# Memory loads in two rooms, their squares issued later, and the first side weights in the weights' own buffers

## The chip, the cores and the metric

The kernel runs on one core of one Trainium2 chip. The time is device microseconds of one execution. Three runs of the kernel before took 1450.09 to 1451.76 us, with a median of 1451.42 us. Engines are named as the profile names them: PE is TensorE (PEld its weight loads), DVE is VectorE, ACT is ScalarE, POOL is GpSimd, and SP is SyncE, whose queue (SPq) issues nearly all DMAs.

## What is computed

One layer of a hybrid encoder on 1024 tokens of width 1024, in float32, in three residual steps. The change lies in the first two.

```
h = x + W_out [ FoX(xn) ++ GLA(xn) ]        xn = RMSNorm(x); one projection W_in feeds both groups
h = h + CrossAttn(RMSNorm(h), RMSNorm(mem)) # 4 heads, QK-norm, 256 memory tokens, weights wq, wkv, wo
y = h + W2 relu(W1 RMSNorm(h))^2            # hidden 4096
```

FoX is causal attention with forget gates, 8 heads of 64, swept over blocks of 128 queries. GLA is gated linear attention, 4 heads. The keys and values of the memory tokens, `memn @ wkv`, depend on `mem` alone, so they can be computed at any time before the cross attention.

## The kernel before, in words

Every float32 product is made of three fp32r products: both operands are split into a high part (rounded, by ACT) and a low part (the rest, by DVE), and PE adds high·high, high·low and low·high (lines 110 to 112, `gemm`). A weight goes through `wsplit`: a DMA brings two blocks of 128 rows into a buffer `raw`, ACT writes `wh` (line 88 without a gain, line 99 with one), DVE writes `wl` (lines 93 and 100). All `wh` and `wl` come from one pool with nine buffers of each.

`raw` buffers come from two places. The weights' own pool (`rawp`, two buffers) exists from the start of the program. With the argument `rooms`, `wsplit` takes every other `raw` from the pool that it is given, as `raw0`. For the side work below that is the pool `side`, which takes the memory of the mixer's inputs: it exists only when PE has done its last product with them. In the trace that is at about 324 us.

The program runs in stages: the mixer's projections with GLA inside (to about 325 us, the values of FoX being the last projection, `W_FV`), the attention of FoX (to about 556 us), the output projection, the cross attention, and the MLP. During FoX a generator `side_work` is stepped between the attention blocks and gives PE further products: first `out_part(0)` (GLA's half of the output projection, left columns: weights `w_out`, split by line 838/839 of the mixer's result `mixg`, stored as `hpd`), then the memory's keys and values (four pieces of `wkv`), then `out_part(1)`.

For the memory, `side_work` loads the transposed memory `memT` in two halves and splits each half into `sh` and `sl` (line 757, done at line 120/121). It also loads the rows of `mem`, takes the mean of their squares on ACT (`mean_square`, line 136) and from it the factors `mev` and `mr` on POOL. All four loads use one buffer `memr`, so each waits for the use of the one before. The product `gx` of two gains (line 747, DVE) is needed when the first keys are scaled (line 783).

The attention itself goes: scores on PE into one of two PSUM banks `s1`, `s2` (660 to 663), row maximum `nm` on DVE (665), exponential `p` on ACT (668), reciprocal `rrec` on DVE (670), scaling on POOL (671), transposes on PE into one of three banks `tr` (696), their split into `pth` (ACT, 117) and `ptl` (DVE, 118), products with the values `va` on PE (704). The values are written to DRAM as `vd` (line 600) and read back as `va` (line 723). The buffers `pth` and `ptl` lie where the values' staging tiles `qn` were, so the first of them waits until the last `vd` store has landed.

The order of the instructions on each engine is fixed when the program is built, by a scheduler that lays the program out with its own estimate of durations. Each engine then takes its rows in that order. `issue_after(x)` tells the scheduler to place what follows behind instruction x.

Of the kernel before, what the change touches and what calls it, by code (L numbers as in the profile page):

```python
# [17 lines left out]
F32 = mybir.dt.float32  # L18
# [3 lines left out]
AF = mybir.ActivationFunctionType  # L22
ALU = mybir.AluOpType
# [5 lines left out]
D = 1024  # L29
M = 256  # L30
P = 128
# [3 lines left out]
EPS = 1e-6  # L35
# [12 lines left out]
def f(ap):  # L48
    return ap.bitcast(F32)


class Layer:
# [14 lines left out]
    def wsplit(self, src, gcols, N=512, lo_pool=0, hi_pool=False, steps=None, beside=None, rooms=None, nraw=2):  # L67


        nc = self.nc  # L70
        kt = src.shape[0] // P
        hs, ls = [], []
        for k0, n in steps or [(k, 2) for k in range(0, kt, 2)]:
            if beside is not None:
                beside(k0, n)
            self.nr += 1
            raw = (self.T(self.rawp, [P, 2, N], F32, "raw") if rooms is None or nraw == 2 and self.nr % 2
                   else self.T(rooms, [P, 2, N], F32, "raw0", bufs=nraw))
            eng = nc.scalar if beside is not None and k0 == 0 else nc.sync
            self.raw_load = eng.dma_start(raw[:, 0:n], src[k0 * P:(k0 + n) * P, :].rearrange("(k p) n -> p k n", p=P))  # L80
            for j in range(n):
                wp = self.wps[self.nw % len(self.wps)]
                self.nw += 1
                wh = self.T(wp, [P, N], F32R, "wh")
                wl = self.T(wp, [P, N], F32R, "wl")
                r = raw[:, j, :]
                if gcols is None:
                    nc.scalar.activation(wh, r, AF.Copy)
                    if lo_pool and (k0 + j) % lo_pool == 0:
                        for c in (slice(0, N // 2), slice(N // 2, N)):  # L90
                            nc.gpsimd.tensor_tensor(wl[:, c], r[:, c], f(wh[:, c]), ALU.subtract)
                    else:
                        nc.vector.tensor_tensor(wl, r, f(wh), ALU.subtract)
                else:
                    g = self.cols[:, gcols + k0 + j:gcols + k0 + j + 1]
                    if hi_pool:
                        nc.gpsimd.tensor_scalar(wh, r, g, 1.0, ALU.mult, ALU.mult)
                    else:
                        nc.scalar.activation(wh, r, AF.Identity, scale=g)  # L99
                    nc.vector.scalar_tensor_tensor(wl, r, g, f(wh), ALU.mult, ALU.subtract)  # L100
                hs.append(wh)
                ls.append(wl)
        return hs, ls
# [169 lines left out]
    def mixer_inputs(self):  # L273
        nc = self.nc
        w_in = self.w_in
        with ExitStack() as st:
# [17 lines left out]

            def token_major(t, W):
                ps = next(banks)
                self.gemm(ps, *([v[t // 4][:, k, t % 4 * P:(t % 4 + 1) * P] for k in range(KT)] for v in (xh, xl)), *W)
                return ps
# [3 lines left out]

            def normed(t, W, dst, g=None):

                ps = token_major(t, W)
                v3 = lambda ap: ap.rearrange("p (h d) -> p h d", h=8)
# [19 lines left out]
            with ExitStack() as s2:  # L326
# [14 lines left out]
                def factors(t):  # L341
# [8 lines left out]
                gbanks = self.two(mmp, 3, trp, 2)  # L350
                W = self.wsplit(w_in[:, W_GQ:W_GQ + 512], C_MIX, hi_pool=True,
                                steps=[(0, 1), (1, 1), (2, 2), (4, 2), (6, 2)], beside=columns(0), rooms=xp, nraw=5)
                ps4 = [next(gbanks) for _ in range(4)]
                for k in range(KT):
                    for i in range(4):
                        wc = slice(i * P, (i + 1) * P)
                        self.gemm(ps4[i], *([w[k][:, wc]] for w in W), *([xs(v, 0, k)] for v in (xh, xl)),
                                  start=k == 0, stop=k == KT - 1)
# [380 lines left out]
    def side_work(self, mp, mmp, trp):  # L739


        nc = self.nc
        v2 = lambda ap: ap.rearrange("p (h d) -> p h d", h=2)
        gk = self.T(mp, [P, 256], F32, "gxk")
        nc.sync.dma_start(self.gx, self.xq_g.partition_broadcast(P))
        nc.sync.dma_start(gk, self.xk_g.partition_broadcast(P))
        nc.vector.scalar_tensor_tensor(self.gx, self.gx, 0.0625, gk, ALU.mult, ALU.mult)
        yield from self.out_part(mp, mmp, 0, ())

        mh, ml = ([self.T(mp, [P, 4, P], F32R, n, bufs=6) for _ in range(4)] for n in ("sh", "sl"))  # L750
        gm = self.cols[:, C_MEM:C_MEM + 8]
        for t in range(2):
            c1 = slice(t, t + 1)
            xt = self.T(mp, [P, 4, M], F32, "memr")
            nc.sync.dma_start(xt, self.memT[:, 4 * t:4 * t + 4, :])
            for j in range(4):
                k, c = 4 * t + j, slice(2 * (j % 2), 2 * (j % 2) + 2)
                self.evac_split(mh[k // 2][:, c, :], ml[k // 2][:, c, :], xt[:, j, :].rearrange("p (t s) -> p t s", t=2), gm[:, k:k + 1])
            xt = self.T(mp, [P, D], F32, "memr")
            nc.sync.dma_start(xt, self.mem[t * P:(t + 1) * P, :])  # L760
            self.mean_square(xt, xt, self.mv[:, c1])
            nc.gpsimd.tensor_scalar(self.mev[:, c1], self.mv[:, c1], EPS, None, ALU.mult)
            nc.gpsimd.tensor_tensor(self.mr[:, c1], self.mv[:, c1], self.mhalf[:, 0:1], ALU.pow)
            yield
        for n in range(4):
            W = self.wsplit(self.wkv[:, n * 512:(n + 1) * 512], None, rooms=mp)
            for t in range(2):
                ps = self.T(mmp, [P, 512], F32, "mm")
                self.gemm(ps, *([m[k // 2][:, 2 * (k % 2) + t, :] for k in range(KT)] for m in (mh, ml)), *W)
                kv = self.T(mp, [P, 2, 512], F32R, "mkv", bufs=2)  # L770
                if n >= 2:
                    vr = self.T(mp, [P, 512], F32, "t2k", bufs=3)
                    nc.scalar.activation(vr, ps, AF.Identity, scale=self.mr[:, t:t + 1])
                    self.evac_split(kv[:, 0, :], kv[:, 1, :], vr)
                    nc.sync.dma_start(self.vmd[:, :, t, (n - 2) * 512:(n - 1) * 512], f(kv))
                    yield
                    continue
                kn = self.T(mp, [P, 512], F32, "t2k", bufs=3)
                kr = self.T(mp, [P, 512], F32, "t2k", bufs=3)
                nc.scalar.activation(kr, ps, AF.Copy)  # L780
                r = self.head_rstd(kr, kn, 2, self.mev[:, t:t + 1])
                nc.vector.tensor_tensor(v2(kn), v2(kr), self.bcast(r, 256), ALU.mult)
                nc.gpsimd.tensor_tensor(v2(kn), v2(kn), self.gx.unsqueeze(1).to_broadcast([P, 2, 256]), ALU.mult)
                yield
                tp = self.T(trp, [P, 512], F32, "tr")
                for j in range(4):
                    nc.tensor.transpose(tp[:, j * P:(j + 1) * P], kn[:, j * P:(j + 1) * P], self.ident)
                self.evac_split(kv[:, 0, :], kv[:, 1, :], tp)
                nc.sync.dma_start(self.kTd[:, :, 4 * n:4 * n + 4, t * P:(t + 1) * P],
                                  f(kv).rearrange("p s (a b) -> p s a b", a=4))  # L790

        yield from self.out_part(mp, mmp, 1, range(2))

    def out_part(self, mp, mmp, n, ks):


        nc = self.nc
        cs = slice(n * 512, (n + 1) * 512)
        W = self.wsplit(self.w_out[512:1024, cs], None, rooms=mp)
        if ks:  # L800
            W = [a + b for a, b in zip(W, self.wsplit(self.w_out[ks[0] * P:(ks[-1] + 1) * P, cs], None, rooms=mp))]
        for half in range(2):
            A = self.split_half(mp, self.mixg, half, 6, range(4))
            if ks:
                A = [a + b for a, b in zip(A, self.split_half(mp, self.mixf, half, 6, ks))]
            for i in range(4):
                ps = self.T(mmp, [P, 512], F32, "mm")
                c = slice(i * P, (i + 1) * P)
                self.gemm(ps, *([w[:, c] for w in w_] for w_ in W), *A)
                xt = self.T(mp, [P, 512], F32, "t2k", bufs=3)  # L810
                nc.sync.dma_start(xt, self.xT[:, 4 * n + i, half * 512:(half + 1) * 512])
                nc.vector.tensor_tensor(xt, ps, xt, ALU.add)
                nc.sync.dma_start(self.hpd[half, 4 * n + i], xt)
                yield
# [539 lines left out]
```

## Time and profile before

| what | value |
|---|---|
| median of three runs | 1451.42 us (1450.09 to 1451.76) |
| profiled execution | 1449.57 us, of which the span of the page is 1447.9 us |
| PE busy | 1425.1 us (98%) |
| DVE, ACT, POOL busy | 938.8 us (65%), 675.2 us (47%), 380.5 us (26%) |
| DMA | 223.93 MB, 155 GB/s mean |
| mean clock granted to PE | 0.994 of full |

The page gives busy time as a share of the span. PE is nearly always busy, so what can be won lies in the few stretches in which it waits or runs at a lower clock. These are found by the windows view (busy time and clock by stretch) and the timelines (what an engine waited for before each instruction, in square brackets).

### The profile page before, as it was taken

The numbers are of one execution on the slowest core, as the hardware profiler recorded it, in microseconds if no ns is written. First come the engines' busy times: TensorE is split into PE (matmuls) and PEld (weight loads), VectorE is DVE, ScalarE is ACT, GpSimd is POOL, SyncE is SP. The second block draws the span as 40 slices with busy tenths as digits, with TensorE's granted clock in tenths as the row PEclk, the third lists the DMA queues.
The fourth block names the chain that finished last, engine by engine and source line by source line (L and its number), as shares of the span: only waits on it lengthen the run. The fifth ranks groups of instructions, "written<-read, shape, count | busy, mean of one in ns | idle before, by whom it ended". The sixth has DMA issues, their size and how long they took to land.

```text
span 1447.9 us, 19165 instructions
## 1 busy us (share of the span) xinstructions
PE 1425.1 (98%) x7036; PEld 1188.0 (82%) x7036; DVE 938.8 (65%) x1342; ACT 675.2 (47%) x1095; POOL 380.5 (26%) x404
## 2 busy tenths in 40 slices
PE   9999999998899999999999999999999999999998
PEld 7788788887788887888888888888888888888887
DVE  5366733428687776656654886655556968778696
ACT  3443441326577755455542264445446745335230
POOL 3235423412233222512212200000000552233454
PEclk9999999999999999999999999999999999999999
DMA  8335520268567634412474114444445835436353
GB/s 312 92 71 134 134 74 0 84 166 269 173 196 210 202 124 138 139 59 88 142 263 184 44 66 175 175 174 189 175 174 207 320 127 189 132 124 225 117 201 119
DMA packets 121165, 223.93 MB, mean 155 GB/s; under 512 B 8912, under 2 KB 54512, under 8 KB 118512
## 3 DMA queue, kind: packets, MB, share of 16 engines
q1 hardware_dynamic: 119776, 218.25, 46.6%
q10 hardware_dynamic: 1296, 4.46, 1.0%
q8 instruction: 56, 0.92, 0.3%
q14 instruction: 37, 0.30, 0.1%
HBM read 150.59 MB, written 72.09 MB: 154 GB/s over the span
## 4 chain that ended last, share of the span: by engine, by line
PE 89%; DMA 5%; ACT 2%; DVE 2%; issue 1%; POOL 0%; SPq 0%; ACTq 0%; DVEq 0%
PE mm L110 15%; PE mm L111 15%; PE mm L112 15%; PE my L110 7%; PE my L112 7%; PE my L111 7%; PE tr L112 4%; PE tr L110 4%; PE tr L111 4%; PE pv L704 2%; PE tr L696 1%; PE s L660 1%; PE s L661 1%; DMA raw<-in_w_in_dram 1%; DMA raw<-in_xattn_wkv_dram 1%
## 5 line engine op out<-in xcount | busy, mean ns | idle before, releaser
L110 PE MATMUL my<-x,g 128*128 128x512 f32 x464 | 180.6, 390 | 0.2 <-ACT h L1197 0.2
L111 PE MATMUL my<-x,g 128*128 128x512 f32 x464 | 180.6, 389 | 0.0
L112 PE MATMUL my<-x,g 128*128 128x512 f32 x464 | 180.5, 389 | 0.0
L111 PE MATMUL mm<-wl,xh 128*128 128x512 f32 x320 | 126.6, 396 | 0.6 <-DVE wl L100 0.6
L110 PE MATMUL mm<-wh,xh 128*128 128x512 f32 x320 | 125.8, 396 | 0.4 <-ACT wh L99 0.3
L112 PE MATMUL mm<-wh,xl 128*128 128x512 f32 x320 | 125.7, 393 | 0.0
L1082 ACT ACTIVATE g<-s 128x1024 fp32r<-128x1024 f32 (+1 forms) x72 | 69.1, 964 | 99.9 <-PE my L112 36.5
L1083 DVE TENSOR_TENSOR g<-raw,g 128x512 fp32r<-128x512 f32 (+3 forms) x72 | 69.2, 964 | 67.9 <-ACT g L1082 67.8
L1082 ACT ACTIVATE g<-raw 128x512 fp32r<-128x512 f32 (+3 forms) x72 | 55.5, 773 | 106.1 <-DMA raw<-in_mlp_w_dram 41.9
L110 PEld LDWEIGHTS my<-x,g 128*128 128x128 f32 x464 | 87.1, 188 | 18.6 <-ACT h L1197 0.6
L111 PEld LDWEIGHTS my<-x,g 128*128 128x128 f32 x464 | 87.1, 188 | 18.3 <-DVE x L1083 0.2
L112 PEld LDWEIGHTS my<-x,g 128*128 128x128 f32 x464 | 87.1, 188 | 18.1
L1109 POOL TENSOR_TENSOR s<-raw 128x384 f32<-128x384 f32 (+1 forms) x20 | 26.4, 1318 | 280.6 <-DMA raw<-in_mlp_w_dram 253.7
L671 POOL TENSOR_SCALAR p<-p,rrec 128x128 f32<-128x128 f32 (+3 forms) x64 | 51.4, 808 | 156.5 <-DVE rrec L670 142.7
L1083 DVE TENSOR_TENSOR g<-s,g 128x1024 fp32r<-128x1024 f32 (+1 forms) x72 | 84.9, 1181 | 9.1 <-ACT g L1082 8.2
L1252 DVE TENSOR_TENSOR x<-x 128x1024 fp32r<-128x1024 f32 (+1 forms) x64 | 77.4, 1230 | 16.0 <-ACT x L1251 15.2
L111 PE MATMUL mm<-x,g 128*128 128x512 f32 x220 | 85.7, 389 | 0.0
L110 PE MATMUL mm<-x,g 128*128 128x512 f32 x220 | 85.6, 389 | 0.0
L112 PE MATMUL mm<-x,g 128*128 128x512 f32 x220 | 85.6, 389 | 0.0
L110 PE MATMUL tr<-x,g 128*128 128x512 f32 x212 | 82.5, 389 | 0.0
L111 PE MATMUL tr<-x,g 128*128 128x512 f32 x212 | 82.5, 389 | 0.0
L112 PE MATMUL tr<-x,g 128*128 128x512 f32 x212 | 82.5, 389 | 0.0
(316 smaller groups left out, 3670.6 us busy)
## 6 DMA issues: line engine op xcount, KB each, us to landing
ud<-h SPq DMA_DIRECT2D x32, 768.0 KB, 3.8
x<-ud SPq DMA_DIRECT2D x48, 512.0 KB, 5.0
raw<-in_mlp_w_dram SPq DMA_DIRECT2D x20, 1024.0 KB, 7.4
raw<-in_mlp_w_dram SPq DMA_DIRECT2D x16, 768.0 KB, 6.2
raw<-in_w_in_dram SPq DMA_DIRECT2D x23, 512.0 KB, 6.8
raw<-in_xattn_wkv_dram SPq DMA_DIRECT2D x16, 512.0 KB, 7.3
od<-o SPq DMA_DIRECT2D x32, 256.0 KB, 4.0
ud<-h SPq DMA_DIRECT2D x32, 256.0 KB, 3.3
```

Source lines behind the costliest of these rows:

```text
L110: mm(ps, lh[k], rh[k], start=start and k == 0, stop=False, **kw)
L111: mm(ps, lh[k], rl[k], start=False, stop=False, **kw)
L112: mm(ps, ll[k], rh[k], start=False, stop=stop and k == n - 1, **kw)
L660: nc.tensor.matmul(ps[:, c], qa[:, ts], ka[:, c], start=True, stop=False)
L661: nc.tensor.matmul(ps[:, c], qb[0:68, ts], kb[0:68, c], start=False, stop=not last)
L671: nc.gpsimd.tensor_scalar(p[:, 0:n], p[:, 0:n], rr, 1.0, ALU.mult, ALU.mult)
L696: t = nc.tensor.transpose(tp[:, c * P:(c + 1) * P], pp[i][:, (2 * b + j) * P:(2 * b + j + 1) * P], self.ident)
L704: nc.tensor.matmul(pv[:, 256 - (js.stop - js.start):256], va[:, 2 * b + j, :], w[:, js], start=b == j == 0 and w is th, stop=b == sb and j ...
L1082: a = self.nc.scalar.activation(hi, src, AF.Copy)
L1083: d = self.nc.vector.tensor_tensor(lo, src, f(hi), ALU.subtract)
L1109: eng.tensor_tensor(s[:, 0], raw[:, 3], raw[:, 2], ALU.add)
L1252: nc.vector.tensor_tensor(lo, f(lo), f(hi), ALU.subtract)
```

## The change

```diff
@@ wsplit @@
-                    nc.scalar.activation(wh, r, AF.Copy)
+                    self.wsplit_hi = nc.scalar.activation(wh, r, AF.Copy).ins
...
-                        nc.vector.tensor_tensor(wl, r, f(wh), ALU.subtract)
+                        self.wsplit_lo = nc.vector.tensor_tensor(wl, r, f(wh), ALU.subtract).ins
@@ side_work @@
-        nc.vector.scalar_tensor_tensor(self.gx, self.gx, 0.0625, gk, ALU.mult, ALU.mult)
         yield from self.out_part(mp, mmp, 0, ())
...
         for t in range(2):
-            c1 = slice(t, t + 1)
-            xt = self.T(mp, [P, 4, M], F32, "memr")
+            xt = self.T(mp, [P, 4, M], F32, "memr", bufs=2)
             nc.sync.dma_start(xt, self.memT[:, 4 * t:4 * t + 4, :])
...
-            xt = self.T(mp, [P, D], F32, "memr")
-            nc.sync.dma_start(xt, self.mem[t * P:(t + 1) * P, :])
-            self.mean_square(xt, xt, self.mv[:, c1])
-            nc.gpsimd.tensor_scalar(self.mev[:, c1], self.mv[:, c1], EPS, None, ALU.mult)
-            nc.gpsimd.tensor_tensor(self.mr[:, c1], self.mv[:, c1], self.mhalf[:, 0:1], ALU.pow)
             yield
+        rows = []
+        for t in range(2):
+            rows.append(self.T(mp, [P, D], F32, "memr", bufs=2))
+            nc.sync.dma_start(rows[t], self.mem[t * P:(t + 1) * P, :])
         for n in range(4):
             W = self.wsplit(self.wkv[:, n * 512:(n + 1) * 512], None, rooms=mp)
+            if n == 0:
+                with self.tc.issue_after(self.wsplit_hi), self.tc.issue_after(self.wsplit_lo):
+                    nc.vector.scalar_tensor_tensor(self.gx, self.gx, 0.0625, gk, ALU.mult, ALU.mult)
+                    for t in range(2):
+                        c1 = slice(t, t + 1)
+                        self.mean_square(rows[t], rows[t], self.mv[:, c1])
+                        nc.gpsimd.tensor_scalar(self.mev[:, c1], self.mv[:, c1], EPS, None, ALU.mult)
+                        nc.gpsimd.tensor_tensor(self.mr[:, c1], self.mv[:, c1], self.mhalf[:, 0:1], ALU.pow)
@@ out_part @@
-        W = self.wsplit(self.w_out[512:1024, cs], None, rooms=mp)
+        W = self.wsplit(self.w_out[512:1024, cs], None, rooms=mp if n else None)
```

The buffer `memr` becomes two. The two halves of `memT` are loaded first, then the two blocks of rows. The rows' squares, with what POOL makes of them, and the product `gx` are placed behind the last conversions of the first piece of `wkv`. The first piece of `w_out` in `out_part(0)` takes both its `raw` buffers from the weights' own pool. No instruction is added or taken away; lines behind 747 move by up to five.

Since the scheduler places everything anew, the order of the attention's rows moves too. Three places matter below. Numbers behind a name count tiles; they differ by one between the two programs (`wh_2794` there is `wh_2793` here).

**ACT at the end of the values' projection.** `w_out` is converted by L88, `p_545` and `p_550` are exponentials of the second block pair, `pth_2863` is the first split of transposed probabilities. Before:

```order
L668 ACTIVATE p_545_2939,rsum_2940<-s_543_2933,nm_2937 128x384
L668 ACTIVATE p_550_2953,rsum_2954<-s_548_2945,nm_2951 128x896
L88 ACTIVATE wh_2794<-raw_500_2792 128x512
L88 ACTIVATE wh_2798<-raw_500_2792 128x512
L88 ACTIVATE wh_2804<-raw_2802 128x512
L88 ACTIVATE wh_2808<-raw_2802 128x512
L117 ACTIVATE pth_2863<-tr_2859 128x384
```

After, the first of the four (`wh_2793`) stands some twenty rows ahead of this piece, and the others in it, ahead of the projection's last row `qn_2758`:

```order
L120 ACTIVATE qn_2729<-mm_2704,xr_82 128x8x64
L88 ACTIVATE wh_2797<-raw_2791 128x512
L88 ACTIVATE wh_2803<-raw_2801 128x512
L668 ACTIVATE p_454_2470,rsum_2471<-s_452_2464,nm_2468 128x256
L88 ACTIVATE wh_2807<-raw_2801 128x512
L668 ACTIVATE p_459_2484,rsum_2485<-s_457_2476,nm_2482 128x768
L120 ACTIVATE qn_2758<-mm_2733,xr_82 128x8x64
```

`p_545`, `p_550` and `pth_2862` now follow each other with nothing between them.

**PE a little later.** `mm_2828` is the first product of the side work, twelve matmuls; `tr_2918` is the fourth bank of transposes, which reuses the first of three. Before, it stands behind all twelve and behind the first product with the values:

```order
L112 MATMUL mm_2828<-sh_2824,wl_2809 128x512
L704 MATMUL pv_2858<-pth_2863,va_2426 128x256
L704 MATMUL pv_2858<-pth_2863,va_2426 128x128
L704 MATMUL pv_2858<-ptl_2864,va_2426 128x128
L704 MATMUL pv_2858<-ptl_2864,va_2426 128x256
L696 MATMUL tr_2918<-ident_75,p_449_2458 128x128
```

After, the twelve are done between the transposes and the scores `s_553` and `s_558`, and the fourth bank comes before the first product with the values:

```order
L663 MATMUL s_558_2970<-maskb_98,identb_93 128x128
L696 MATMUL tr_2917<-ident_75,p_449_2458 128x128
L696 MATMUL tr_2917<-ident_75,p_459_2484 128x128 x2
L660 MATMUL s_589_3103<-ka_2848,qa_2846 128x256
L661 MATMUL s_589_3103<-kb_2849,qb_2847 128x256
L663 LDWEIGHTS identb_93
L663 MATMUL s_589_3103<-maskb_98,identb_93 128x128
L696 MATMUL tr_2985<-ident_75,p_545_2938 128x128
L110 MATMUL mm_2873<-sh_2811,wh_2793 128x512
```

So the second product of the side work, `mm_2873`, has moved up, and the transposes of `tr_2917` stand right behind `s_558`.

**ACT at the memory's first rows.** L120 splits `memT`, L136 takes the squares of the rows, `p_649` and `p_654` are exponentials for which PE's score banks wait. Before:

```order
L120 ACTIVATE sh_3570<-memr_3577,cols_74 128x256 x2
L707 ACTIVATE ol_3083<-pv_3031 64x256
L117 ACTIVATE pth_3223<-tr_3218 128x512
L117 ACTIVATE pth_3236<-tr_3231 128x512
L117 ACTIVATE pth_3248<-tr_3244 128x384
L136 ACTIVATE memr_3587,ss_3589<-memr_3587 128x1024
L707 ACTIVATE ol_3181<-pv_3168 64x256
L668 ACTIVATE p_649_3296,rsum_3297<-s_647_3288,nm_3294 128x896
L668 ACTIVATE p_654_3308,rsum_3309<-s_652_3302,nm_3306 128x512
```

After, the first squares stand here, behind the last conversion of the first piece of `wkv`:

```order
L88 ACTIVATE wh_3762<-raw_793_3756 128x512
L120 ACTIVATE sh_3570<-memr_3667,cols_74 128x256 x2
L88 ACTIVATE wh_3768<-raw_3766 128x512
L120 ACTIVATE sh_3571<-memr_3667,cols_74 128x256 x2
L88 ACTIVATE wh_3772<-raw_3766 128x512
L136 ACTIVATE memr_3732,ss_3777<-memr_3732 128x1024
L843 ACTIVATE sh_4886<-mixg_120 128x512
L88 ACTIVATE wh_4085<-raw_890_4083 128x512
```

`p_649` and `p_654` are now more than twenty rows ahead of them. The second block's squares stand where they stood, between `p_740` (before: `p_742`) and the copy of the first keys.

## The prediction

> **What bounds the kernel now.** I read the page first, then PE's windows in steps of 4 us, then the timelines of PE, ACT, DVE and SP where PE is not full.
>
> ```profile
> span 1447.9 us, 19165 instructions
> PE 1425.1 (98%) x7036; PEld 1188.0 (82%) x7036; DVE 938.8 (65%) x1342; ACT 675.2 (47%) x1095; POOL 380.5 (26%) x404
> PE 89%; DMA 5%; ACT 2%; DVE 2%; issue 1%; POOL 0%; SPq 0%; ACTq 0%; DVEq 0%
> ```
>
> PE bounds the program, so only two things can save time: stretches in which PE waits, and stretches in which its clock is low. In the windows view (columns: stretch, length, PE busy with its instructions, granted clock, DMA share, GB/s) both occur at two places:
>
> ```profile
> 324.00:328.00 4.00, 3.04 (x21) 1.00 0.43 83
> 328.00:332.00 4.00, 2.53 (x10) 1.00 0.95 319
> 332.00:336.00 4.00, 2.88 (x8) 0.59 1.06 379
> 336.00:340.00 4.00, 4.00 (x17) 0.55 1.07 402
> 340.00:344.00 4.00, 3.62 (x21) 1.00 1.03 212
> 364.00:368.00 4.00, 3.69 (x20) 1.00 0.70 224
> 368.00:372.00 4.00, 0.42 (x1) 0.79 0.23 68
> 372.00:376.00 4.00, 4.00 (x17) 0.50 0.70 211
> 376.00:380.00 4.00, 4.00 (x22) 0.86 1.05 318
> ```
>
> No other window shows a clock under 1.00, but for the last of the span, in which PE has nothing left to do. Place 1 (324 to 344): PE waits 0.96 + 1.47 + 1.12 + 0.38 = 3.9 us. The clock takes away 4 x (0.41 + 0.45) = 3.4 us, of which some 0.3 falls into waits: 3.1. Together **7.0 us**. Place 2 (364 to 380): waits 0.31 + 3.58 = 3.9 us; clock 4 x (0.21 + 0.50 + 0.14) = 3.4 us, of which 0.65 falls into the wait: 2.75. Together **6.6 us**. A low clock costs nearly as much as the wait before it.
>
> PE's timeline says who was waited for (start, us, engine, line, count, then idle time before it and its releaser):
>
> ```profile
> 326.11 1.39 PE L696 MATMUL tr<-ident,p 128*128 128x128 f32 x11 [0.46 <-DVE qn L121]
> 328.80 0.50 PE L660 MATMUL s<-ka,qa 128*128 128x512 f32 x1 [1.29 <-ACT p L668]
> 331.57 0.50 PE L110 MATMUL mm<-sh,wh 128*128 128x512 f32 x1 [0.50 <-ACT wh L88]
> 333.43 0.80 PE L112 MATMUL mm<-sh,wl 128*128 128x512 f32 x1 [1.12 <-DVE wl L93]
> 371.58 0.79 PE L660 MATMUL s<-ka,qa 128*128 128x512 f32 x1 [3.90 <-ACT p L668]
> ```
>
> Behind them stand DMAs, in the timelines of ACT and DVE and in the chain of waits (last two rows):
>
> ```profile
> 330.89 2.19 ACT L88 ACTIVATE wh<-raw 128x512 fp32r<-128x512 f32 x4 [1.16 <-DMA raw<-in_w_out_dram]
> 333.74 1.47 ACT L117 ACTIVATE pth<-tr 128x384 fp32r<-128x384 f32 x3 [0.66 <-DMA vd<-qn]
> 368.85 1.06 ACT L136 ACTIVATE memr<-memr 128x1024 f32<-128x1024 f32 x1 [4.44 <-DMA memr<-in_mem_dram]
> 370.43 1.01 ACT L668 ACTIVATE p<-s,nm 128x896 f32<-128x896 f32 x1
> 328.61 0.42 DVE L747 SCALAR_TENSOR_TENSOR gx<-gx,gxk 128x256 f32<-128x256 f32 x1 [1.05 <-DMA gxk<-in_xattn_k_norm_g_dram]
> 326.48 7.08 DMA vd<-qn
> 362.86 5.91 DMA memr<-in_mem_dram
> ```
>
> Place 2 is simple. The squares L136 stand on ACT ahead of the exponential that PE's score bank needs, and they wait 4.44 us for rows whose load could be issued only at 362.86, when the one `memr` was free. Place 1 is a mixture: late `w_out` conversions, DVE held by `gx`, six splits ahead of an exponential, and the last `vd` store, which lands at 326.48 + 7.08 = 333.56 and frees `pth`.
>
> **The change, part by part.**
>
> *Squares behind the conversions, two rooms.* The work is the same: two L136 and three small POOL rows each, four loads on SP. The first L136 no longer stands ahead of `p_649`. Its load is issued at about the old place on SP, between two stores of `hpd`, so by the old 5.91 us it lands near 365, and the squares now come only after the last `wkv` conversions. In the trace of before those are at
>
> ```profile
> 389.14 0.62 ACT L88 ACTIVATE wh<-raw 128x512 fp32r<-128x512 f32 x1
> 394.75 1.06 ACT L136 ACTIVATE memr<-memr 128x1024 f32<-128x1024 f32 x1 [2.27 <-DMA memr<-in_mem_dram]
> 392.00:396.00 4.00, 4.00 (x21) 1.00 0.73 262
> 396.00:400.00 4.00, 4.00 (x26) 1.00 0.33 86
> ```
>
> so the load has some 20 us to spare. Place 2's 6.6 us go: **-6.6**. The second L136 keeps its row and its room still waits for the second `memT` split, so ACT waits some 2.27 us there again. It cost nothing, since PE was full in both windows (the last two rows, 4.00 of 4.00): products of the side work covered it. If that cover were gone the price would be those 2.27 us, and with a fall of the clock some 3 more. Queued behind it are the first keys' copy, `p_745` and `p_750`, and PE's score banks wait for these.
>
> *First weights in their own buffers.* Two loads of `w_out` move from 324.73 (the first of them) to SP's places near 270, where before one of `w_out` and one of `wkv` stood. Their four conversions, 2.19 us on ACT and 2.5 us on DVE, now lie before 324, where both engines have gaps, and PE is full; the one window from 276 to 324 below 4.00 is
>
> ```profile
> 312.00:316.00 4.00, 3.93 (x20) 1.00 1.08 320
> ```
>
> One conversion on DVE also stands ahead of a GLA mask, which may start up to 1.7 us later; PE reads that mask some ten microseconds on. Cost: nothing. At place 1 the waits of 0.50 and 1.12 us for `wh` and `wl` go, and the twelve products of `mm_2827` fill the 1.29 us before `s_553`. In exchange, two loads of `wkv` are issued where the conversions free the buffers (320 to 323), and two more follow behind the `vd` store.
>
> *Where the stall goes.* The new order lets PE reach the fourth bank of transposes early, and that bank needs `pth` and `ptl` of the first, hence the last `vd` store. Walked by rows: PE ends the common part at 325.65; one product 0.23; eleven transposes from 326.1 to 327.5 as before; six products to 328.9, since `p_545` frees the bank at 328.65 as before; `s_553` 0.6, five products 1.15, `s_558` 1.1: 331.7. There `tr_2917` waits: store landed 333.56, `pth` to 334.2, `ptl` 0.5 to 334.8 by
>
> ```profile
> 343.71 0.53 DVE L118 TENSOR_TENSOR ptl<-tr,pth 128x384 fp32r<-128x384 f32 x1
> 340.85 0.68 DVE L812 TENSOR_TENSOR t2k<-mm,t2k 128x512 f32<-128x512 f32 x1
> ```
>
> so PE stands 3.1 us. Then `mm_2873` needs its bank, emptied by a `t2k` row that DVE now takes behind two `ptl` (334.8 + 0.6 + 0.6 = 336.0), while PE is there at 335.7: 0.3. With 0.35 before 329 and up to 1 for a POOL scaling behind, PE waits 3.8 to 4.7 us. If the clock falls as before that is 3.1 more: 6.9 to 7.8 against 7.0 now. If it does not, 3.8 to 4.7.
>
> The landing itself is bounded by what shares the queue:
>
> ```profile
> t2k<-in_xT_dram SPq DMA_DIRECT2D x3, 256.0 KB, 6.2
> raw<-in_w_out_dram SPq DMA_DIRECT2D x1, 512.0 KB
> vd<-qn SPq DMA_DIRECT2D x1, 512.0 KB
> memr<-in_memT_dram SPq DMA_DIRECT2D x1, 512.0 KB
> raw<-in_xattn_wkv_dram SPq DMA_DIRECT2D x1, 512.0 KB
> ```
>
> Now 1024 KB go ahead of it (one `raw`, two `t2k`), then 768 (three `t2k`); 1280 KB follow it before it lands, then 2048. At the 319 to 379 KB/us of the windows, strict order makes it 0.7 us earlier, equal sharing (512 KB more in all) 1.4 us later. I take 0.5 us earlier, nearer to strict order, since the store at the end of its row got only what was left by then. So place 1 with a fallen clock becomes about 6.8: **-0.2**, bounds -3.6 and +1.5.
>
> *`gx` behind the conversions.* DVE no longer waits 1.05 us for `gxk`; its 0.42 us move to a place before the first keys' scaling. No row of PE waited on it directly; it is inside place 1.
>
> *The rest of the attention.* The order changes to about 556 us, with the same rows. Waits there are small:
>
> ```profile
> 404.00:408.00 4.00, 3.31 (x23) 1.00 0.64 180
> 552.00:556.00 4.00, 2.28 (x18) 1.00 0.81 275
> ```
>
> are the two largest. With both stops shortened PE runs closer to ACT and DVE; I take **+0.4**, bounds -1.5 and +2.5.
>
> Sum: -6.6 - 0.2 + 0.4 = -6.4 us. Against the profiled execution's own 1449.57 that is 1443.2; it lay 1.85 below the median of the runs shown, so as a median 1451.42 - 6.4 = **1445.0**.
>
> **Rivals.**
>
> 1. *The clock holds at place 1.* It was low for about 6.8 us each time, and only after these two stops; the new stop is one of 3.1 us where place 2 had 3.9. Against it: at place 1 the clock fell with single waits of at most 1.29 us. If it holds, 3.1 us more are saved: 1441.9.
> The Trainium skill, page "TensorE: Matmul & The Clock Gate", section "What's actually happening", has the clock halved after at least one idle window of about 3.4 us on a free-running count. By that, a stop of 3.1 us need not halve it, and the phase decides; the first fall here, with no single wait above 1.29 us, speaks against reading it as one unbroken wait. Hence only a small chance for this rival.
>
> 2. *Only the memory part acts.* The `vd` store lands 1.4 us later by equal sharing and the attention's new order costs its 2.5: 1451.42 - 6.6 + 1.5 + 2.5 = 1448.8. For it: four loads of 512 KB stand behind the store.
>
> 3. *The stop moves to the second squares.* ACT waits its 2.27 us or more for the second rows, and this time PE is not covered: 2.3 to 3.9 of wait and 2.75 of clock give back 5 to 6.6: about 1451. Against it: the full windows from 392 to 400.
>
> 4. *Slower: the late load ahead of the exponentials.* ACT now takes four `wkv` conversions (2.19 us) ahead of `p_560` and `p_591`. The load of `raw_783` is issued near 329; PE needs `p_560` at about 340.3, so by 1.1 for the exponential and 2.2 for the conversions it must land by 337.0. The row
>
> ```profile
> 348.67 0.63 ACT L88 ACTIVATE wh<-raw 128x512 fp32r<-128x512 f32 x1 [3.98 <-DMA raw<-in_xattn_wkv_dram]
> ```
>
> shows how such a load can hold ACT. Each microsecond past 337.0 is one of PE, and about 3 more if the clock falls anew. To outweigh 6.4 us and be 2.9 slower it must land some 6 us late, at 343, 14 us after its issue, with the clock fallen: 1454.5. The longest landing on the chain is the load of that row,
>
> ```profile
> 339.77 8.87 DMA raw<-in_xattn_wkv_dram
> ```
>
> so it is unlikely.
>
> That the change does not do what it says is excluded by the order for the squares and the weights; only what it costs elsewhere is open.
>
> **How the numbers follow.** Forecast 0.52; rival 1 0.17; rival 2 0.13; rival 3 0.09; rival 4 0.09. A measurement of this kernel can tell about 0.2% (2.9 us) from no change. The forecast and rivals 1 and 2 mostly end faster (rival 2 at 2.6 us below, half of it): faster 0.75; same is rival 3 and half of rival 2, 0.16; slower is rival 4, 0.09. The range runs from rival 1 less 1.4 to rival 2 and a little more: 1440.5 to 1450. The forecast's own range, by its bounds without the clock, is 1443 to 1448.
>
> **What would show it.** At place 2 of the new profile no wait of ACT for `memr` ahead of the exponentials and the clock at 1.00: then the 6.6 us are right. The first row of `tr` after `s_558` waiting for `ptl`, with `pth` waiting for `vd`, and a clock near 0.5 behind it: then place 1 is right; a clock of 1.00 there is rival 1. A wait of PE for `p` near 385 to 395 is rival 3, one near 340 with ACT waiting for `raw<-in_xattn_wkv_dram` is rival 4. The prediction is wrong if PE's waits between 324 and 556 sum to as much as now.

## The result and the profile after

| | before | after | ratio |
|---|---|---|---|
| first series, medians (6 and 6 runs) | 1451.59 us | 1439.82 us | 0.9923 [0.9907, 0.9939] |
| again, medians (16 and 6 runs) | 1449.63 us | 1439.92 us | 0.9929 [0.9913, 0.9945] |
| profiled executions | 1449.57 us | 1440.62 us | |

The change is faster by 9.7 to 11.8 us, and by 8.95 us between the two profiled executions. The forecast was 6.4 us. The time lies 0.7 us under the range. Over all series the median of before was 1449.6 to 1451.6 us, and the base of the forecast, 1451.42 us, lies inside that. So its sum was too small, by 3.3 to 5.4 us.

The windows view of after, the same stretches as for before (the columns shown are stretch, length, PE busy with its instructions, granted clock, DMA share, GB/s):

```profile
324.00:328.00 4.00, 3.89 (x23) 1.00 0.88 248
328.00:332.00 4.00, 3.56 (x17) 1.00 1.08 379
332.00:336.00 4.00, 1.11 (x4) 0.71 1.04 399
336.00:340.00 4.00, 4.00 (x12) 0.50 1.03 387
340.00:344.00 4.00, 4.00 (x26) 0.93 1.06 256
364.00:368.00 4.00, 4.00 (x27) 1.00 0.84 212
368.00:372.00 4.00, 4.00 (x25) 1.00 0.99 305
372.00:376.00 4.00, 4.00 (x29) 1.00 0.82 190
376.00:380.00 4.00, 4.00 (x28) 1.00 0.33 106
```

Place 2 (364 to 380) is gone, wait and clock. Place 1 (324 to 344) is now one stop: 0.11 + 0.44 + 2.89 = 3.4 us of waits. The clock takes 4 x (0.29 + 0.50 + 0.07) = 3.4, some 0.5 of it inside the stop, so place 1 costs 6.3 us where it cost 7.0. The timelines of PE, ACT and SP name the stop:

```profile
334.80 0.87 PE L696 MATMUL tr<-ident,p 128*128 128x128 f32 x3 [3.24 <-DVE ptl L118]
333.57 1.47 ACT L117 ACTIVATE pth<-tr 128x384 fp32r<-128x384 f32 x3 [4.31 <-DMA vd<-qn]
326.23 0.53 SPq L600 DMA_DIRECT2D vd<-qn  x1
333.46 0.81 SPq L723 DMA_DIRECT2D va<-vd  x2
```

PE waits for `ptl`, this for `pth`, and `pth` for the last `vd` store, issued at 326.23. SP issues the load of `va` as soon as that store has landed: 333.46, 7.2 us later. This pair of rows is used below as a measure of the landing.

Two of the prediction's fears can be read off too. The late `wkv` load (rival 4) held ACT for 0.98 us and PE not at all; the second squares no longer wait for their rows:

```profile
337.18 2.19 ACT L88 ACTIVATE wh<-raw 128x512 fp32r<-128x512 f32 x4 [0.98 <-DMA raw<-in_xattn_wkv_dram]
378.81 1.05 ACT L136 ACTIVATE memr<-memr 128x1024 f32<-128x1024 f32 x1
384.33 1.06 ACT L136 ACTIVATE memr<-memr 128x1024 f32<-128x1024 f32 x1
```

A common clock through both traces: the same product of the out projection's left half stands at 505.47 us before and at 495.64 us after, and the last product of the program at 1442.95 and 1434.02 us. So 9.8 us are won by 505 us, of which 0.4 lie ahead of 313 us, and at the end 8.9 are left. The waits of PE behind that product do not explain the difference of 0.9: they sum to 4.94 us before and 5.07 after. Its cause stays open; the product need not stand behind the same work in both orders.

### The profile page after: what moved, and what is told of

Same layout as the page of the kernel before. It is cut to its first block, busy times and chain, and to the rows that moved or that the text cites. A ratio compares the mean times of both kernels' runs of the same rounds, so it can differ in the third digit from the quotient of the medians.

```text
span 1438.9 us, 19147 instructions
## 1 busy us (share of the span) xinstructions
PE 1421.3 (99%) x7036; PEld 1185.4 (82%) x7036; DVE 937.8 (65%) x1342; ACT 675.2 (47%) x1095; POOL 385.2 (27%) x404
## 4 chain that ended last, share of the span: by engine, by line
PE 89%; DMA 4%; ACT 3%; DVE 2%; issue 2%; POOL 0%; SPq 0%; ACTq 0%; DVEq 0%; POOLq 0%
PE mm L110 15%; PE mm L111 15%; PE mm L112 15%; PE my L110 7%; PE my L112 7%; PE my L111 7%; PE tr L112 3%; PE tr L111 3%; PE tr L110 3%; PE pv L704 2%; PE tr L696 2%; PE s L660 1%; PE s L661 1%; DMA ud<-h 1%; DMA raw<-in_mlp_w_dram 1%
```

## The experiments

Sixteen runs were made, two of them of the kernel before and the change again. All ratios are to the kernel before, run beside them.

| run | median us | ratio |
|---|---|---|
| before again | 1449.56 | 1.0002 [0.9988, 1.0016] |
| memory's part alone | 1447.51 | 0.9986 [0.9972, 1.0001] |
| weights' part alone | 1450.03 | 0.9995 [0.9980, 1.0010] |
| change, `pth`/`ptl` moved | 1448.70 | 0.9987 [0.9972, 1.0001] |
| change again | 1439.92 | 0.9929 [0.9913, 0.9945] |
| `wq` last: before | 1448.64 | 0.9985 [0.9973, 0.9998] |
| `wq` last: weights' part | 1446.18 | 0.9969 [0.9955, 0.9983] |
| `wq` last: memory's part | 1444.09 | 0.9959 [0.9943, 0.9975] |
| `wq` last: change | 1440.30 | 0.9930 [0.9914, 0.9947] |
| `wq` last: change, `pth`/`ptl` moved | 1445.07 | 0.9961 [0.9949, 0.9974] |
| the same, `va` first | 1446.30 | 0.9969 [0.9955, 0.9982] |
| `wq` last: change, `va` first | 1442.92 | 0.9951 [0.9936, 0.9965] |
| change, `vd` in rows | 1441.41 | 0.9935 [0.9921, 0.9948] |
| `wq` last, `va` first, `vd` in rows | 1443.25 | 0.9950 [0.9937, 0.9963] |
| `wq` last: change, `t2k` behind the store | 1443.87 | 0.9949 [0.9932, 0.9966] |
| the same, `va` first | 1451.82 | 1.0003 [0.9988, 1.0019] |

**The kernel before and the change, each again.** No edit.

> The kernel before, once more, to see how much two executions of one program differ and where. If the whole gap between the forecast (6.4 us) and the medians (11.8 us) were in the new program, the second profile shows the same stalls and the same falls of the clock at 324 to 344 and 364 to 380 us, and the runs lie within 1 us of 1449.6. If part of the gap is that the profiled execution of before was a lucky one, the runs lie between 1448 and 1454 with a median near 1451.5, and the second profile differs from the first by a fall of the clock (about 3.4 us for each stretch of some 7 us at half the clock) or by the length of a DMA wait, at a place that can be named.

> The change itself once more, beside the kernel before on the same chip. If the 11.8 us by medians are the change's, the ratio is 0.991 to 0.993 again and the profile shows place 2 full, the stop of about 3.2 us for ptl at 331.5 us, and the end of the attention (540 to 550 us) with its three small waits of 1.2, 0.5 and 0.5 us and the clock at 1.00. If part of them was a sample of before with many falls of the clock, the ratio is 0.993 to 0.995 (8 to 9.5 us, the difference of the two profiled executions).

Before shows the same two stops, waits of 3.9 and 3.6 us, each with 3.4 us lost to the clock. Its runs spread from 1447.3 to 1453.8 us, so its first profiled execution was a typical one. The change repeats its time. Its place 1 does not repeat:

```profile
328.00:332.00 4.00, 3.89 (x18) 1.00 1.06 340
332.00:336.00 4.00, 1.81 (x12) 1.00 1.06 380
336.00:340.00 4.00, 4.00 (x12) 0.57 1.01 380
```

Here the waits are 0.11 + 2.19 = 2.3 us and the clock takes 4 x 0.43 = 1.7: 4.0 us instead of 6.3.

**The parts alone.**

```diff
 # memory's part alone: the change, with
-        W = self.wsplit(self.w_out[512:1024, cs], None, rooms=mp if n else None)
+        W = self.wsplit(self.w_out[512:1024, cs], None, rooms=mp)
 # weights' part alone: the kernel before, with the opposite edit
```

> The memory's two rooms and the squares behind the conversions alone; the first piece of w_out takes its buffers as before. The prediction: place 2 (364 to 380 us) is full at clock 1.00, place 1 (324 to 344 us) keeps about 7 us of waits and slow clock, 1449.6 - 6.6 = 1443.0 us as a profiled execution and about 0.9955 of before. Rival: the weights' part carries more than the 0.2 us of the forecast, because the whole change gained 11.8 us by medians: then this kernel gains no more than 6.6, and e2_weights_only the other 2 to 5. Other rival: the rest of the gain lies in the order of the attention that the memory's part brings; then this kernel alone reaches 0.992 to 0.993.

> The first weights' buffers alone; the memory's loads and squares as before. The prediction: place 1 keeps a stop of some 3 us for the last vd store and a fall of the clock behind it, gain 0.2 us (bounds -3.6 and +1.5), place 2 keeps its wait of 3.9 us and its fall of the clock: 1449.4 us, ratio 0.998 to 1.001. Rival: place 1 itself got shorter by 1 to 3 us, ratio 0.997 to 0.998. Since pth here lies where it lies in before, the wait for the vd store must show again.

Neither part alone gained what either theory said, though place 2 was full in the first. (The profiled execution of the memory's part took 1451.52 us, 4.0 more than its median.) The trace showed a third place, the end of the attention. The windows and then PE's timeline of the memory's part alone:

```profile
552.00:556.00 4.00, 0.32 (x2) 0.86 0.66 206
556.00:560.00 4.00, 4.00 (x18) 0.50 0.02 6
560.00:564.00 4.00, 4.00 (x15) 0.79 0.62 197
```

```profile
550.53 0.50 PE L704 MATMUL pv<-pth,va 128*128 128x256 f32 x2 [1.34 <-DVE mixf L710]
555.73 0.80 PE L704 MATMUL pv<-pth,va 128*128 128x256 f32 x2 [3.68 <-DVE mixf L710]
```

and PE's timeline at the same place in the change:

```profile
544.40 0.55 PE L696 MATMUL tr<-ident,p 128*128 128x128 f32 x3 [1.22 <-DVE ptl L118]
545.45 0.51 PE L704 MATMUL pv<-pth,va 128*128 128x256 f32 x2 [0.50 <-DVE mixf L710]
547.49 0.51 PE L704 MATMUL pv<-ptl,va 128*128 128x256 f32 x2 [0.47 <-DVE ptl L118]
```

5.0 us of waits and 3.4 us of clock stand against 2.2 us and none. The scheduler had found two endings. Before and the change got the one, both parts alone the other. In the bad ending a conversion of `wq` (line 99), whose load is late, stands on ACT ahead of the copy `ol`, as the timelines of ACT and PE of the next kernel show (both parts alone have the same pair of rows, at 553.72 and 554.58 us):

```profile
547.30 0.72 ACT L99 ACTIVATE wh<-raw,cols 128x512 fp32r<-128x512 f32 x1 [1.23 <-DMA raw<-in_xattn_wq_dram]
548.05 0.38 ACT L707 ACTIVATE ol<-pv 64x256 f32<-64x256 f32 x1
549.31 0.80 PE L704 MATMUL pv<-pth,va 128*128 128x256 f32 x2 [3.85 <-DVE mixf L710]
```

**`pth` and `ptl` off the staging tiles.** The pool of `pth` and `ptl` overlaps the staging pool; in front of it the pool of `ol`, made 2 KB larger, takes that memory.

```diff
-            pt = self.open(st, "foxpt", 5)
-            olp = self.open(st, "foxol", 3)
+            olp = self.open(st, "foxol", 5)
+            pt = self.open(st, "foxpt", 5)
```

> The change, with the pool of the attention's small outputs (ol, five buffers instead of three) laid in front of the pool of pth and ptl, so that these no longer lie on the values' staging tiles: nothing of theirs waits for the last vd store. If the stop of 3.2 us at 331.5 us is that store and the fall of the clock follows from the stop, both go: 3.4 of waits and 2.9 of clock, 1440.6 - 6.3 = 1434.3 us and about 0.988 of before. Rival: the late wkv load (ACT took it at 337.2 us, ahead of the exponential p_560) takes the stop's place, a wait of 1 to 3 us for p at about 336 to 340 us, with or without a fall of the clock: 1436 to 1441 us. Third: the stop was not the store, then nothing moves (1440).

The stop for `ptl` went. PE then waited for `va`, which is read back from `vd` and comes behind the same store:

```profile
339.52 0.45 PE L704 MATMUL pv<-pth,va 128*128 128x256 f32 x2 [2.46 <-DMA va<-vd]
```

And the bad ending came with it (the rows just above). The wait for the store had hidden the wait of its reader. This profiled execution, 1444.47 us, is the fastest of the twelve; what the others lost beyond it, 4.2 us at the median, no trace shows.

**One ending for all.** The conversions of `wq` are placed behind the last `ol` on ACT, in five kernels.

```diff
-                nc.scalar.activation(ol, pv[64:128, :], AF.Copy)
+                self.last_ol = nc.scalar.activation(ol, pv[64:128, :], AF.Copy).ins
...
-                Ws[n] = self.wsplit(self.wq[:, n * 512:(n + 1) * 512], C_XAT)
+                with self.tc.issue_after(self.last_ol): Ws[n] = self.wsplit(self.wq[:, n * 512:(n + 1) * 512], C_XAT)
```

> The change, with the conversions of wq placed behind the attention's last copy of ol on ACT. In the change those conversions stand between the copies and cost PE some 2.2 us of small waits at the end, with no fall of the clock. Theory: the wait for wq's load is not on PE's path there, so the time stays within 1 us of the change itself. Rival: the conversions' 2 us hold the splits pth and the copies, and 1 to 2 us are saved.

> The memory's part alone, as in the run of it before, and the conversions of wq placed behind the last copy of ol. That run lost 3.7 us at 552 us to PE's wait for mixf, because ACT had taken a wq conversion whose load was late ahead of a copy of ol, and some 3 us to the fall of the clock behind it. If these are the cause, the stop goes, the clock stays at 1.00 from 548 to 564 us, and the time falls by 5 to 7 us against that run: profiled about 1445, by medians 1442 to 1443 and a ratio near 0.995, which is the prediction's 6.6 us. If the end of the attention is slow for another reason (too little side work left for PE), PE still waits there 3 to 5 us and the ratio stays near 0.9985.

> The kernel before with the conversions of wq placed behind the attention's last copy of ol, as the ground line for the parts. As in the change, this order alone should be worth less than 1 us here: ratio 0.999 to 1.0005, with both stops (324 to 344, 364 to 380 us) and their falls of the clock as before. If the order at the end is worth more than thought, 0.997 to 0.998, and the memory's part alone (1444.1, 5.5 us under before in its run) owes that much to the end and not to its own place.

> The first weights' buffers alone, with the conversions of wq behind the last copy of ol. If the two parts add up (whole change with this end 1440.3, memory's part with this end 1444.1), the weights are worth 3.8 us: 1445.5 to 1446, ratio 0.997 to 0.998, with place 2 still at some 5 to 6.6 us of wait and slow clock and the stop at 549 us gone. If the weights only pay where the memory's part has worsened place 1 (9 us there in its profile instead of 7), the ratio is 0.999 to 1.001, which is the prediction's 0.2 us.

> The change with pth and ptl clear of the values' staging tiles and the conversions of wq behind the last copy of ol: both stops named so far are gone. The first run without the wait for the vd store kept no fall of the clock at place 1 but waited 2.5 us there for va, and lost 3.85 us and a fall of the clock at 549 us. If the second is cured, 5 to 6 us less: about 1438.5 as profiled, 1441 to 1443 by medians where the clock falls at place 1 in some executions. Rival: the stop at the end stays, because the copies of ol wait for something else, and the time stays at 1444 to 1449.

The stop at the end is gone from the memory's part; small waits are left there, and the clock holds (windows):

```profile
548.00:552.00 4.00, 1.94 (x14) 1.00 0.66 205
552.00:556.00 4.00, 4.00 (x26) 1.00 0.33 84
```

and its time falls by 0.0027 of the whole, 3.9 us (between the profiled executions 1451.5 to 1445.8, 5.7 us). For the change nothing moves, as expected: its ending was already the good one. Now the four kernels differ in the two parts alone:

| `wq` last | without memory's part | with it | memory's part is worth |
|---|---|---|---|
| without weights' part | 0.9985 | 0.9959 | 0.0026, 3.8 us |
| with it | 0.9969 | 0.9930 | 0.0039, 5.7 us |
| weights' part is worth | 0.0016, 2.3 us | 0.0029, 4.2 us | both: 0.0055, 8.0 us |

Each ratio is known to 0.0013 to 0.0017, so a difference of two to some 0.002, or 3 us. The memory's part is clear. The weights' part is plainly not the 0.2 us of the forecast in one row, and not settled in the other. That before with `wq` last is 2 us faster than before was not expected; the interval reaches to 0.3 us.

The profile of the weights' part with `wq` last shows one reason why the memory's part is worth less than 6.6 us on the average: without it place 2 does not always cost as much. Here PE waited there for `p` as before, but 1.3 us, and no clock fell. Waits and lost clock from 360 to 384 us, added up, are 7.3 and 7.0 us in the two profiles of before, 5.3 in the weights' part alone, 5.0 in before with `wq` last and 2.0 here. Its windows and PE's timeline:

```profile
360.00:364.00 4.00, 3.42 (x20) 1.00 0.80 311
364.00:368.00 4.00, 2.73 (x12) 1.00 0.89 272
368.00:372.00 4.00, 3.87 (x21) 1.00 0.85 250
```

```profile
364.72 0.50 PE L660 MATMUL s<-ka,qa 128*128 128x512 f32 x1 [1.30 <-ACT p L668]
```

The weights' part may be worth more beside the memory's for a reason at place 1. In the memory's part with `wq` last the windows from 324 to 344 us hold 1.15 + 1.04 + 0.84 + 2.22 + 0.43 = 5.7 us of waits, half of it for `va`, and the clock takes 3.4 us in two falls. The first run of the memory's part has 6.0 and 5.1 us (all counted to 348 us), where before has 3.9 to 4.7 and 3.4. So in these profiles the memory's part alone makes place 1 worse by 1 to 4 us, where its expectation had it unchanged. The wait for `va` in PE's timeline:

```profile
340.43 0.45 PE L704 MATMUL pv<-pth,va 128*128 128x256 f32 x2 [2.65 <-DMA va<-vd]
```

With `pth` and `ptl` moved and `wq` last the time is worse than the change's. The wait for `va` remains, and this time the clock fell. PE's timeline and the windows:

```profile
342.11 0.69 PE L704 MATMUL pv<-pth,va 128*128 128x256 f32 x2 [2.85 <-DMA va<-vd]
```

```profile
340.00:344.00 4.00, 1.89 (x7) 0.68 1.06 346
344.00:348.00 4.00, 4.00 (x12) 0.50 0.96 247
```

**What makes the store late.** First the loads behind it are taken away: `memT` and `wkv` queue behind the first load of `va` on SP. Then the shape of `vd` is changed, so that a store writes 4096 bytes in a piece and not 512. Then `t2k` is taken from ahead of it.

```diff
 # va first
-                nc.sync.dma_start(f(A[4]), self.vd[:, h])
+                va = nc.sync.dma_start(f(A[4]), self.vd[:, h]).ins; self.va0 = self.va0 if h else va
...
-            nc.sync.dma_start(xt, self.memT[:, 4 * t:4 * t + 4, :])
+            with self.tc.issue_after(self.va0): nc.sync.dma_start(xt, self.memT[:, 4 * t:4 * t + 4, :])
...
-            W = self.wsplit(self.wkv[:, n * 512:(n + 1) * 512], None, rooms=mp)
+            with self.tc.issue_after(self.va0): W = self.wsplit(self.wkv[:, n * 512:(n + 1) * 512], None, rooms=mp)
 # vd in rows (store and load are indexed to match)
-            self.vd = self.T(dram, [P, 8, NT, P], F32, "vd")
+            self.vd = self.T(dram, [P, NT, 8, P], F32, "vd")
...
 # t2k behind the store (vd_last is the last store of vd)
-                nc.sync.dma_start(xt, self.xT[:, 4 * n + i, half * 512:(half + 1) * 512])
+                with self.tc.issue_after(self.vd_last): nc.sync.dma_start(xt, self.xT[:, 4 * n + i, half * 512:(half + 1) * 512])
```

> The change with pth and ptl clear of the staging tiles, wq's conversions at the end, and SP's loads of memT and wkv queued behind the first load of va. In the run without this, PE waited 2.85 us for va (loaded back from vd) at 342 us. If 2 MB of loads issued right behind the vd store are what makes store and load land late, the store lands near 330 instead of 333.4 us, va near 333, and no stop of over 1 us and no fall of the clock is left from 324 to 350 us: 1433 to 1435 us, ratio 0.988 to 0.990. If store and load are slow by themselves (pieces of 512 B), the wait for va stays at 2 to 3 us: 1441 to 1445. Third: the wkv conversions, now later on ACT, leave PE without side work and it waits for wh or wl at 345 to 375 us: about 1438.

> The change with wq's conversions at the end and SP's loads of memT and wkv queued behind the first load of va; pth and ptl still wait for the last vd store. Tests the prediction's step on what shares the queue with the store: with 768 KB ahead of it and nothing behind it, 1280 KB at 380 KB/us after 324.3 us make it land at 328 to 330 us, before PE reaches the transposes at 331.5 us; the stop of 1.8 to 3.6 us goes with its fall of the clock, 1440.3 - 6 = 1434 us, ratio 0.989. If the loads behind the store cost it nothing, it lands at 333.4 us as now and the time stays at 1440. Third, as in the run beside this: wkv is late and PE waits for its side work at 345 to 375 us, 1438.

> The change with the order of the two middle axes of vd swapped in DRAM, so that a store writes 4096 bytes in one piece for each partition (before: eight pieces of 512) and the load of va reads eight pieces of 512 (before: one of 4096). The order on PE, ACT and DVE is that of the change. If the last store takes 6 to 7 us because of its small pieces, it lands 2.5 to 4 us after its issue, near 330 us, and the stop for ptl at 331.5 us goes with its fall of the clock; then va, now in small pieces behind 2 MB of other loads, comes late and PE waits 2 to 4 us for it at 337 to 343 us: 1437 to 1441, ratio 0.991 to 0.994. If the store's time is a fixed cost, it lands at 333 us again and the time is 1440 or, with the slower va, more. If va is no slower, 1434 and 0.989.

> The same swap on the run with va ahead of the loads of memT and wkv (1442.9 there): order on PE and ACT as there. If the pieces are the cause, the store lands near 330 us, va is issued at once and lands by 334 to 336 us, and at place 1 at most 1 us of wait is left with no fall of the clock: 5 to 6 us under that run, 1437, ratio 0.991. If the store's time is a fixed cost, its landing stays at 333 us, and the time at 1443 or later by the slower load.

> The change with wq's conversions at the end and the three loads of t2k queued behind the last vd store on SP; the scheduler now puts both loads of memT and one of wkv, 1536 KB, ahead of the store instead of the 768 KB of t2k. If what is queued ahead decides the landing, the store takes longer than 7 us from its issue, by up to 768 KB at 380 KB/us, 2 us more, and place 1 gets worse: 1442 to 1444. If only a fixed cost decides, it lands 6 to 7 us after its issue and the time is near 1440.

> The run with va ahead of memT and wkv, with the loads of t2k queued behind the last vd store too: nothing but 128 KB stands ahead of the store, 768 KB behind it. If the transfers ahead decide, it lands 768 KB at 380 KB/us, 2 us, earlier than the 5.7 to 7.0 us of those runs, 4 to 5 us after its issue, near 330.5 us; the stop for ptl goes and with it the fall of the clock at place 1, unless t2k, now later, makes DVE late for the one bank of products. If the cost is fixed, it lands at 332 to 333 us again.

SP's timelines give the issue of the last store and, by the load of `va`, its landing. In this order: the change with `wq` last and `va` first, then with `t2k` behind the store, then with both:

```profile
326.01 0.52 SPq L600 DMA_DIRECT2D vd<-qn  x1
332.97 0.81 SPq L723 DMA_DIRECT2D va<-vd  x2
```

```profile
328.12 0.92 SPq L600 DMA_DIRECT2D vd<-qn  x1
338.38 0.80 SPq L723 DMA_DIRECT2D va<-vd  x2
```

```profile
325.84 0.51 SPq L600 DMA_DIRECT2D vd<-qn  x1
329.92 0.80 SPq L723 DMA_DIRECT2D va<-vd  x2
```

| loaded in the 3 us ahead of the store | from issue to landing |
|---|---|
| 128 KB (both) | 4.1 us |
| 768 KB of `t2k` and 128: `memT` and `wkv` behind it (change, three profiles) | 7.2, 5.9, 7.2 us |
| 768 KB of `t2k` and 128: nothing behind it (`va` first, two profiles) | 5.7, 7.0 us |
| 768 KB of `t2k` and 128, `vd` in rows: loads behind it; nothing behind it | 8.2; 5.8 us |
| 1024 KB of `w_out` and `t2k`, and 128 (before, three profiles) | 7.1, 7.0, 6.9 us |
| 1536 KB of `memT` and `wkv`, and 128 (`t2k` behind the store) | 10.3 us |

The landing follows what is queued ahead, though its two ends rest on one profile each. Of what is queued behind and of the size of the pieces no effect shows beyond the spread among like runs, 1.3 us for the change and 2.4 us with `vd` in rows. None of these kernels beat the change. Only one landing came early, that with both edits, and it was paid elsewhere; with `va` first alone the store landed no earlier. With `t2k` behind the store it landed late, and ACT waited for `wkv` ahead of an exponential: the prediction's rival 4, with 6.1 us of PE. With both edits the stop for `ptl` went, but PE stood 2.6 us at the next product with the values (the profile names no releaser). Later the second squares waited for their rows, and PE for what ACT had behind them, the copy of the keys (line 785): rival 3. A second stop of the same kind came 40 us later, behind a late `wkv` load, and the clock fell at all three. The timelines of PE and ACT, of the one and of the other kernel:

```profile
339.87 0.58 PE L660 MATMUL s<-ka,qa 128*128 128x256 f32 x1 [6.10 <-ACT p L668]
336.96 2.19 ACT L88 ACTIVATE wh<-raw 128x512 fp32r<-128x512 f32 x4 [5.51 <-DMA raw<-in_xattn_wkv_dram]
```

```profile
335.52 0.66 PE L704 MATMUL pv<-pth,va 128*128 128x256 f32 x2 [2.60 <-issue]
397.95 1.06 ACT L136 ACTIVATE memr<-memr 128x1024 f32<-128x1024 f32 x1 [5.63 <-DMA memr<-in_mem_dram]
399.64 0.79 PE L110 MATMUL mm<-wh,sh 128*128 128x512 f32 x1 [4.86 <-ACT t2k L785]
437.30 0.63 ACT L88 ACTIVATE wh<-raw 128x512 fp32r<-128x512 f32 x1 [4.33 <-DMA raw<-in_xattn_wkv_dram]
439.50 0.79 PE L110 MATMUL mm<-wh,sh 128*128 128x512 f32 x1 [4.13 <-ACT t2k L785]
```

## Why the prediction was right and wrong

**Place 2, -6.6: right in mechanism and in the profiled pair.** Its four windows are full at clock 1.00. By medians the memory's part is worth 3.8 to 5.7 us, and in other profiles without it place 2 lost less (down to 2.0 us, above).

**The second squares' wait of 2.27 us, to stay at no cost:** wrong that it stays, right that it costs nothing.

**Place 1, -0.2: the step that failed.** The walk named the right row (the transposes `tr`), the right releaser (`ptl`, `pth`, the last `vd` store) and the stop: 3.1 us forecast, 3.24 in the first profile. But the two small waits behind it (0.3 for `t2k`, up to 1 for POOL) did not come. PE ran at half its clock there, so DVE and POOL had the time; that reading is argued from the rows, not tested. And the clock's fall was taken at its full 3.1 us. Four profiles with the change's order of PE at place 1 (the change twice, with `wq` last, with `vd` in rows) had waits of 3.4, 2.3, 3.8 and 3.9 us and a clock that took 3.4, 1.7, 1.7 and 1.7; three of before (twice, with `wq` last) had 3.9, 3.9 and 4.7 us and 3.4 each time. The windows of the change with `wq` last:

```profile
332.00:336.00 4.00, 0.40 (x2) 0.94 1.08 401
336.00:340.00 4.00, 3.92 (x15) 0.63 0.99 343
```

Waits and lost clock added up, place 1 cost 7.3 to 8.1 us in the profiles of before and 4.0 to 6.8 in those four, some 2 us less on the average and not 0.2. The weights' part measured 2.3 us beside the old memory's part, which is not clear of 0.2, and 4.2 beside the new one, which is. The prediction's lower bound of -3.6 was nearer to this than the value taken. Why the clock falls for the longer or the shorter time is open.

**The landing, 0.5 us earlier by strict order:** the direction, less ahead and so earlier, agrees with the last runs, and the size was not seen: 6.9 to 7.1 us from issue to landing in three profiles of before, 5.9 to 7.2 in three of the change.

**The rest of the attention, +0.4:** between 380 and 505 us PE waited 2.25 us before and 1.57 after, so about -0.7. That lies inside the bounds of -1.5 and +2.5, but the sign was wrong, and this term is 1.1 us of what the sum lacked. With some 2 us of place 1 it makes up 3 of the 3.3 to 5.4 us. The bounds were too narrow for what a new order can bring: in three of the first kernels it was the bad ending, with some 6 us more of waits and clock. That before and the change share the good one is nothing that the prediction had looked at.

**Rivals.** Rival 1 (the clock holds at place 1, 1441.9) came nearest: the clock fell, but in three of four profiles for half as long. Rivals 3 and 4 did not occur in the change and both occurred in its variants, at the rows named.

## What to carry to other kernels

Price a fall of the clock as a chance and not as a constant, and take the ground for a small gain from several executions. Where a scheduler lays everything out anew, look at every place whose order can flip, and hold such a place fixed before two parts are compared. Where a transfer lands late, look at what is queued ahead of it, and ask what the moved loads are needed for: here the one early landing gained nothing.

## What was not expected of the hardware

In 18 profiles the clock fell 28 times between 300 and 600 us. The time at half the clock, summed from windows of 2 us, was 6.8 us in 17 of these and 3.4 us in 11, and nothing between. So a fall costs PE 3.4 or 1.7 us where PE has work. It came behind a single wait of 6.1 us, but in before also where none was above 1.29 us, and it did not come behind the wait of 2.46 us for `va`. So in these profiles the length of a single wait does not tell whether it comes. The Trainium skill, page "TensorE: Matmul & The Clock Gate", section "What's actually happening", has a free-running window of about 3.4 us. The steps of 3.4 us agree with it, and so does the same stop costing once 3.4 and once 1.7 us.
